# Expert routing on one core: the exponential of the expert weights moved behind the key selections and tied to a gelu

## The chip, the cores and the metric

The kernel runs on one core of a Trainium2 chip. The metric is the device time of one execution in microseconds (us). A core has five engines with a queue each: PE (TensorE: matrix products, weight loads apart as PEld), DVE (VectorE), ACT (ScalarE: activation functions), POOL (GpSimd) and SP (SyncE, which here only issues transfers). Each engine works through its queue strictly in order; semaphores join the queues.

## The reference, cut to what matters

The network has two layers over 256 context and 256 latent tokens of width 1024. Each layer ends in a product-key expert feed-forward block, 16384 experts of which each of 8 heads uses 16 for each token:

```python
s1, i1 = lax.top_k(s[:, :, 0], PEER_TOPK)
s2, i2 = lax.top_k(s[:, :, 1], PEER_TOPK)
cand = (s1[..., :, None] + s2[..., None, :]).reshape(...)
cidx = (i1[..., :, None] * PEER_NKEYS + i2[..., None, :]).reshape(...)
top_s, pos = lax.top_k(cand, PEER_TOPK)
eidx = jnp.take_along_axis(cidx, pos, axis=-1)
g = jax.nn.softmax(top_s, axis=-1)
act = jax.nn.gelu(jnp.einsum('td,thkd->thk', xc, u[eidx]), approximate=False)
coef = g * act
return jnp.einsum('thk,thkd->td', coef, v[eidx])
```

The change concerns the exponential inside `softmax(top_s)`, on 128 tokens x 128 weights at a time.

## The kernel before, in words

The expert block doesn't gather rows of `u`. It multiplies all of them with the tokens, 128 experts in a step, in `u_step`: a step loads one 128x1024 block of `u` (SP, tile `wr`, four buffers), splits it in a high and a low part for exact products (`whi` by ACT, `wlo` by POOL, three buffers each, L364 and L365), runs 24 matmuls of the three partial products into PSUM (`pu`, two buffers in layer 0, three in layer 1), takes the gelu on ACT (`gel`, L538) and stores it in DRAM from the ACT queue. There are 128 steps in a layer (the U stage). In layer 0 they cover 512 tokens, but the first 22 steps only the 256 latent ones, because attention did the context half earlier; in layer 1 they cover 256 tokens.

Beside it `route_tile` works out, for 128 tokens at a time (four tiles in layer 0, two in layer 1), which experts count and with what weight. That is nearly all DVE work: the best 16 of 128 scores for 16 key sets, the sums `cand`, the best 16 of 256 for 8 heads, the subtraction of the maximum (L910, into `e = g[:, 2]`), then for each of the two key indices (x = 0 and 1) three passes over 128x2048 elements (`eq`, L921, L925, L927), then the sum `z`, its reciprocal and the division of `e` (L932 to L934, L941). Three PE transposes (L945, `ptr`) turn the result, DVE casts it (`gT`, L947), and 16 groups of one-hot tiles A and B (L975 to L978) feed matmuls (`pw`) that scatter the weights into a dense matrix, which goes to DRAM by way of ACT (`stg`) and a transfer. The last tile of layer 0 takes a shorter way: `index` turns it into row numbers for gathers in the next stage (the V stage).

The order of PE and of DVE in the U stage is the order in which the program is written out. It is woven by hand: `route_tile` is a generator that yields a planned cost after each piece, and `pace` runs it on at the middle and at the end of each step of U. A tile of dense routing costs 93.5 units by the plan. Layer 0 has 3 x 93.5 + 52 = 332.5 units over 112 steps (its half steps count half), layer 1 has 187 over 120. After the end of each step from step 24 on, layer 0 also writes out one product for the second layer's modulation vectors (`mj`, L166, on DVE), whose operand `wm` comes by an SP transfer.

The order of ACT and of SP isn't written out. A scheduler of the framework orders their instructions by its own model of when operands are ready. `issue_after(ins)` forbids it one thing: an instruction written in that block can't stand ahead of `ins` in their engine's queue. `self.gel` is the latest gelu that `u_step` has written:

```python
self.mm3(p, w, h, t0, t1, range(4))
if mid:
    mid()
self.mm3(p, w, h, t0, t1, range(4, C))
g = self.w.tile([P, T], F32, tag="gel", name="gel", bufs=3)[:, :n]
self.gel = nc.scalar.activation(g, p, AF.Gelu)
nc.scalar.dma_start(self.Gd[l][j][:, t0:t1], g)
```

So a piece of routing that is written in the middle of step j sees the gelu of step j-1, one at the end of step j sees that of step j. ACT holds one set of function tables at a time; exp and gelu are in different sets, so each exponential among the gelus comes with one table load before it and one after it.

Of the kernel before, what the change touches and what calls it, by code (L numbers as in the profile page):

```python
# [14 lines left out]
AF = mybir.ActivationFunctionType  # L15
# [94 lines left out]
class Trunk:  # L110
# [767 lines left out]
    def route_tile(self, l, ps, rp, s, it, Wd):  # L878
        nc = self.nc
# [29 lines left out]
        e = g[:, 2]  # L909
# [9 lines left out]
        for x in range(2):  # L919
            eq = rp.tile([P, HEADS, TOPK, TOPK], F32, tag="cand", name="eq")  # L920
            V.tensor_tensor(eq.rearrange("p h k j -> p (h k) j"),  # L921
                            abf[:, x].rearrange("p h k -> p (h k)")[:, :, None].to_broadcast([P, P, TOPK]),
                            self.iota[:, None, :TOPK].to_broadcast([P, P, TOPK]), op=OP.is_equal)
            yield 2.2
            V.tensor_tensor(eq, eq, sifp[:, :, x, None, :].to_broadcast([P, HEADS, TOPK, TOPK]), op=OP.mult)  # L925
            yield 2.2
            V.tensor_reduce(g[:, x], eq, axis=AX.X, op=OP.add)  # L927
            if x == 0:
                nc.scalar.activation(e, e, AF.Exp)
            yield 2.2  # L930
        z = rp.tile([P, HEADS], F32, tag="z", name="z")
        V.tensor_reduce(z, e, axis=AX.X, op=OP.add)  # L932
        V.reciprocal(z, z)
# [32 lines left out]
        for t0 in range(0, P, TG):  # L966
            stg = rp.tile([P, NK, TG], F32, tag="stg", name="stg", bufs=2)
            for u0 in range(t0, t0 + TG, HB):
# [3 lines left out]
                x = [gT[:, y, u0:u0 + HB, None].to_broadcast(sh) for y in range(4)]  # L972
# [623 lines left out]
```

## Time and profile before

| what | us |
|---|---|
| median of 3 runs | 2804.37 |
| lowest and highest of them | 2802.23, 2816.68 |
| the profiled execution, its own time | 2819.22 |
| its span, first to last instruction | 2817.4 |
| PE busy with matmuls in it | 2644.6 |
| DVE busy | 2080.1 |
| POOL busy | 1300.8 |
| ACT busy | 1176.5 |

All views below are of that one profiled execution, whose own time is 14.85 us above the median of the runs.

### The profile page before, as it was taken

The page shows a single profiled execution, that of the slowest core. Times are in us where ns is not written, and L with a number is a line of the kernel's source. Part 1 is how long each engine was busy: PE and PEld are TensorE (multiplying, and loading weights), DVE is VectorE, ACT ScalarE, POOL GpSimd, SP SyncE. Part 2 cuts the span into 40 slices and gives each one's busy share as a digit, 9 for nine tenths or more (in the row PEclk, how much of TensorE's full clock was granted, in tenths as well). Part 3 has the DMA queues.
Part 4 walks back from the last instruction along what each step waited for, and adds up shares of the span by engine and source line. Part 5 has one row for each costly group of instructions (what it writes and reads, how often), then busy time and mean ns, then how long its engine had stood idle before and what let it go on. Part 6 is the DMA issues. An engine that isn't in the chain of part 4 may idle for free.

```text
span 2817.4 us, 46000 instructions
## 1 busy us (share of the span) xinstructions
PE 2644.6 (94%) x17403; PEld 2407.1 (85%) x17403; DVE 2080.1 (74%) x3689; ACT 1176.5 (42%) x1953; POOL 1300.8 (46%) x730
## 2 busy tenths in 40 slices
PE   8889999999899999999999999987999899999998
PEld 3667898887777777789999999977999799999998
DVE  5898764839958959515988878688939929577776
ACT  3445433434224233333333333464445445444444
POOL 3433440755445445446777763243578688400000
PEclk9989999999999999999999999999999999999999
DMA  7342262557548668558999998314578678888885
GB/s 259 131 133 77 89 215 83 172 191 250 198 165 257 222 228 269 189 185 293 353 358 385 376 346 328 111 47 143 176 214 261 191 221 261 304 284 278 278 278 171
DMA packets 223566, 631.58 MB, mean 224 GB/s; under 512 B 28480, under 2 KB 84464, under 8 KB 218736
## 3 DMA queue, kind: packets, MB, share of 16 engines
q1 hardware_dynamic: 148880, 468.03, 49.0%
q0 software_dynamic: 33888, 109.75, 11.5%
q10 hardware_dynamic: 40576, 50.87, 5.0%
q8 instruction: 136, 2.23, 0.3%
q14 instruction: 86, 0.70, 0.1%
HBM read 535.28 MB, written 93.33 MB: 223 GB/s over the span
## 4 chain that ended last, share of the span: by engine, by line
PE 61%; DVE 25%; DMA 5%; issue 3%; ACT 3%; POOL 3%; SPq 0%; ACTq 0%; DVEq 0%; POOLq 0%
PE y L1169 26%; PE pu L373 7%; PE pu L375 7%; PE pu L374 7%; DVE mj L166 3%; DVE B L977 2%; DVE B L976 2%; DVE A L975 2%; POOL wlo L365 2%; DVE B L978 2%; DMA gr<-Gd 1%; PE pq L373 1%; PE pq L375 1%; PE pq L374 1%; PE pw L958 1%
## 5 line engine op out<-in xcount | busy, mean ns | idle before, releaser
L365 POOL TENSOR_TENSOR wlo<-wr,whi 128x1024 fp32r<-128x1024 f32 x306 | 801.2, 2624 | 697.7 <-ACT whi L364 562.0
L364 ACT ACTIVATE whi<-wr 128x1024 fp32r<-128x1024 f32 x575 | 608.7, 1059 | 905.3 <-PE pu L374 493.9
L1169 PE MATMUL y<-gh,whi 128*128 128x256 f32 (+1 forms) x2072 | 635.3, 309 | 12.8 <-ACT gh L352 11.0
L1169 PE MATMUL y<-gl,whi 128*128 128x256 f32 (+1 forms) x2072 | 639.6, 309 | 4.3 <-DVE gl L353 3.8
L1169 PE MATMUL y<-gh,wlo 128*128 128x256 f32 (+1 forms) x2072 | 638.2, 308 | 0.5 <-DVE wlo L365 0.5
L365 DVE TENSOR_TENSOR wlo<-wr,whi 128x1024 fp32r<-128x1024 f32 x291 | 358.4, 1232 | 294.1 <-ACT whi L364 268.4
L373 PE MATMUL pu<-hh,whi 128*128 128x512 f32 (+1 forms) x1024 | 394.8, 386 | 21.1 <-ACT gel L538 21.1
L1169 PEld LDWEIGHTS y<-gh,whi 128*128 128x128 f32 x2072 | 389.1, 188 | 17.3 <-ACT gh L352 14.8
L1169 PEld LDWEIGHTS y<-gl,whi 128*128 128x128 f32 x2072 | 394.9, 191 | 7.5 <-DVE gl L353 7.3
L1169 PEld LDWEIGHTS y<-gh,wlo 128*128 128x128 f32 x2072 | 390.5, 188 | 0.7 <-DVE wlo L365 0.7
L375 PE MATMUL pu<-hh,wlo 128*128 128x512 f32 (+1 forms) x1024 | 385.7, 377 | 3.7 <-POOL wlo L365 3.7
L374 PE MATMUL pu<-hl,whi 128*128 128x512 f32 (+1 forms) x1024 | 383.5, 375 | 0.0
L373 PE MATMUL pu<-h,whi 128*128 128x256 f32 x1024 | 296.5, 290 | 6.6 <-ACT whi L364 6.6
L375 PE MATMUL pu<-h,wlo 128*128 128x256 f32 x1024 | 290.8, 284 | 7.8 <-POOL wlo L365 7.8
L374 PE MATMUL pu<-h,whi 128*128 128x256 f32 x1024 | 290.0, 283 | 0.0
L373 PEld LDWEIGHTS pu<-hh,whi 128*128 128x128 f32 x1024 | 195.7, 191 | 53.6 <-ACT gel L538 23.0
L375 PEld LDWEIGHTS pu<-hh,wlo 128*128 128x128 f32 x1024 | 195.2, 191 | 41.1 <-POOL wlo L365 4.9
L374 PEld LDWEIGHTS pu<-hl,whi 128*128 128x128 f32 x1024 | 196.1, 192 | 31.6
L166 DVE SCALAR_TENSOR_TENSOR mj<-wm,cb 128x1024 bf16<-128x1024 f32 x128 | 206.1, 1610 | 1.3 <-DMA wm<-in_wmodT 0.9
L375 PEld LDWEIGHTS pu<-h,wlo 128*128 128x128 f32 x1024 | 195.7, 191 | 9.3 <-POOL wlo L365 9.3
L373 PEld LDWEIGHTS pu<-h,whi 128*128 128x128 f32 x1024 | 196.2, 192 | 6.8 <-ACT whi L364 6.8
L352 ACT ACTIVATE gh<-G 128x384 fp32r<-128x384 f32 (+1 forms) x250 | 115.6, 462 | 195.3 <-DVE G L1109 177.7
(378 smaller groups left out, 4907.1 us busy)
## 6 DMA issues: line engine op xcount, KB each, us to landing
wr<-in_uT SPq DMA_DIRECT2D x278, 512.0 KB, 3.9
wr<-in_vT SPq DMA_DIRECT2D x256, 512.0 KB, 5.0
wm<-in_wmodT SPq DMA_DIRECT2D x80, 512.0 KB, 4.0
Wd<-stg POOLq DMA_DIRECT2D x40, 1024.0 KB, 7.7
Gd<-gel ACTq DMA_DIRECT2D x106, 256.0 KB, 2.7
wb<-Wd SPq DMA_DIRECT2D x16, 1536.0 KB, 10.8
gr<-Gd SPq DMA_DIRECT2D x128, 192.0 KB, 6.7
Gd<-gel ACTq DMA_DIRECT2D x172, 128.0 KB, 3.5
```

What stands on the lines that cost most here:

```text
L166: x = nc.vector.scalar_tensor_tensor(j, rs[i], 1.0, self.cb[:, s], op0=OP.mult, op1=OP.mult, accum_out=self.mv[l][n // C][:, n % C, s:s + 1])
L352: self.nc.scalar.activation(hi, x, AF.Copy)
L364: nc.scalar.activation(hi, r, AF.Copy)
L365: (lo_engine or nc.vector).tensor_tensor(lo, r, hi.bitcast(F32), op=OP.subtract)
L373: nc.tensor.matmul(out, whi[:, s], hh[:, c, t0:t1], start=c == 0, stop=False)
L374: nc.tensor.matmul(out, whi[:, s], hl[:, c, t0:t1], start=False, stop=False)
L375: nc.tensor.matmul(out, wlo[:, s], hh[:, c, t0:t1], start=False, stop=c == C - 1)
L975: V.tensor_tensor(Av, io, x[0], op=OP.is_equal)
L976: V.tensor_tensor(Bv[1], io, x[1], op=OP.is_equal)
L977: V.tensor_tensor(Bv[0], Bv[1], x[2], op=OP.mult)
L978: V.tensor_tensor(Bv[1], Bv[1], x[3], op=OP.mult)
L1169: nc.tensor.matmul(y[:, n0:n1], w[:, s], g[:, n0:n1], start=first and x == 0, stop=False, skip_group_check=True)
```

## The change

The exponential leaves the loop over the two key indices and is written once after it, just ahead of the sum that needs it, inside a block that forbids the scheduler to put it ahead of the latest gelu.

```diff
             V.tensor_tensor(eq, eq, sifp[:, :, x, None, :].to_broadcast([P, HEADS, TOPK, TOPK]), op=OP.mult)
             yield 2.2
             V.tensor_reduce(g[:, x], eq, axis=AX.X, op=OP.add)
-            if x == 0:
-                nc.scalar.activation(e, e, AF.Exp)
             yield 2.2
+        with self.tc.issue_after(self.gel.ins):
+            nc.scalar.activation(e, e, AF.Exp)
         z = rp.tile([P, HEADS], F32, tag="z", name="z")
         V.tensor_reduce(z, e, axis=AX.X, op=OP.add)
         V.reciprocal(z, z)
```

## Rows read from the trace of the kernel before

**Rows 1.** The page's first part: busy time of each engine, share, instructions.

```profile
PE 2644.6 (94%) x17403; PEld 2407.1 (85%) x17403; DVE 2080.1 (74%) x3689; ACT 1176.5 (42%) x1953; POOL 1300.8 (46%) x730
```

**Rows 2.** The exponential's line: durations in ns; under it, idle ahead of it.

```profile
L929 ACT ACT_TABLE_LOAD  x6: 1283/1283/1283, 530.7 to 2221.4; - x6
L929 ACT ACTIVATE g<-g x6: 309/310/317, 532.7 to 2231.9; 128x128 f32<-128x128 f32 x6
...
  DVE g L910: 44.7, 6
```

**Rows 3.** Waits: who waited for whom, us in total, times, longest.

```profile
DVE gT L947 <- PE ptr L945: 204.1, 5, 51.9
...
PE pu L373 <- ACT gel L538: 21.1, 4, 8.1
...
PE pu L373 <- ACT whi L364: 6.6, 1, 6.6
```

**Rows 4.** Timeline of ACT, second tile of layer 0: start, duration, idle before.

```profile
731.56 0.58 ACT L538 ACTIVATE gel<-pu 128x512 f32<-128x512 f32 x1
737.00 0.58 ACT L538 ACTIVATE gel<-pu 128x512 f32<-128x512 f32 x1
...
737.97 1.28 ACT L929 ACT_TABLE_LOAD   x1 [0.39 <-ACT gel L538]
752.89 0.31 ACT L929 ACTIVATE g<-g 128x128 f32<-128x128 f32 x1 [13.64 <-DVE g L910]
...
763.81 0.58 ACT L538 ACTIVATE gel<-pu 128x512 f32<-128x512 f32 x1
```

**Rows 5.** Timeline of PE there: the first matmul after its pause.

```profile
755.16 0.79 PE L373 MATMUL pu<-hh,whi 128*128 128x512 f32 x1 [8.11 <-ACT gel L538]
```

**Rows 6.** Stretches there: length, busy us (count) by engine, granted clock, transfers.

```profile
750.00:755.00 5.00, 0.00 (x0) 0.00 (x0) 4.93 (x15) 2.08 (x3) 0.00 (x0) 0.50 0.39 156
755.00:760.00 5.00, 4.84 (x12) 3.83 (x13) 5.00 (x4) 2.49 (x4) 3.87 (x2) 0.53 0.46 141
```

**Rows 7.** Timeline of ACT: gelus around the exponentials of tiles three and four.

```profile
946.29 0.58 ACT L538 ACTIVATE gel<-pu 128x512 f32<-128x512 f32 x1
...
972.01 0.58 ACT L538 ACTIVATE gel<-pu 128x512 f32<-128x512 f32 x1
...
1132.99 0.58 ACT L538 ACTIVATE gel<-pu 128x512 f32<-128x512 f32 x1
...
1155.95 0.58 ACT L538 ACTIVATE gel<-pu 128x512 f32<-128x512 f32 x1
```

**Rows 8.** Timeline of ACT: gelus around the second exponential of layer 1.

```profile
2217.83 0.37 ACT L538 ACTIVATE gel<-pu 128x256 f32<-128x256 f32 x1
...
2220.69 0.36 ACT L538 ACTIVATE gel<-pu 128x256 f32<-128x256 f32 x1
...
2242.79 0.36 ACT L538 ACTIVATE gel<-pu 128x256 f32<-128x256 f32 x1
```

**Rows 9.** Timeline of POOL around the first exponential of each layer.

```profile
530.12 2.40 POOL L365 TENSOR_TENSOR wlo<-wr,whi 128x1024 fp32r<-128x1024 f32 x1 [0.47 <-ACT whi L364]
535.75 29.41 POOL L365 TENSOR_TENSOR wlo<-wr,whi 128x1024 fp32r<-128x1024 f32 x9 [3.23 <-ACT whi L364]
...
2025.90 27.37 POOL L365 TENSOR_TENSOR wlo<-wr,whi 128x1024 fp32r<-128x1024 f32 x9 [3.52 <-ACT whi L364]
```

**Rows 10.** Timeline of ACT: the gelu of step 57 in layer 0.

```profile
807.33 0.58 ACT L538 ACTIVATE gel<-pu 128x512 f32<-128x512 f32 x1
```

**Rows 11.** Timeline of PE: the second tile's transposes.

```profile
811.79 0.49 PE L945 MATMUL ptr<-ident,g 128*128 128x128 f32 x3
```

**Rows 12.** Timeline of DVE: from the second tile's sum to what follows.

```profile
778.16 0.27 DVE L932 TENSOR_REDUCE z<-g 128x8 f32<-128x128 f32 x1
...
779.17 1.22 DVE L166 SCALAR_TENSOR_TENSOR mj<-wm,cb 128x1024 bf16<-128x1024 f32 x1
```

**Rows 13.** Timeline of ACT: the V stage's first gelu, late in layer 0's U stage.

```profile
1173.78 0.42 ACT L1105 ACTIVATE gr<-gr 128x256 f32<-128x256 f32 x1 [6.38 <-DMA gr<-Gd]
```

## The prediction

> **What bounds the kernel now.** I read the page's first part, then the line of the exponential, the waits, the timelines of ACT, PE, DVE and POOL around each of the six exponentials, and stretches of a few us there. PE is busy for 94% of the span [rows 1], so only what makes PE stand still, or run at its lower clock, is worth anything.
>
> In the U stage a step of layer 0 takes 5.44 us from gelu to gelu (737.00 - 731.56 [rows 4]), one of layer 1 2.86 us (2220.69 - 2217.83 [rows 8]). The exponential is cheap: six times a 1.283 us table load and 0.31 us of work. But ACT stood idle 44.7 us in front of the six, waiting for DVE's subtraction L910 [rows 2]. At the second tile ACT loads the tables at 737.97 and can compute only at 752.89 [rows 4]. All that time nothing else on ACT runs, and behind the exponential in its queue stand the gelus, which free PE's accumulators, and the splits `whi`, which feed POOL and PE. PE runs on until both accumulators are full, stands for 8.11 us until the gelu comes [rows 5], and then works at a granted clock of 0.50 to 0.53, the lower of its two levels (1.2 of 2.4 GHz), in a stretch whose predecessor had no matmul [rows 6].
>
> Why is ACT there so early? Gelus counted, the exponential at 752.89 stands behind the gelu of step 46. By the yields it is written at unit 37.0 of a tile (16.8 + 2.2 + 13.6 for the selections and sums, 4.4 for two passes), for the second tile at (93.5 + 37.0)/332.5 x 112 + 11 = step 55.0 (the 11 are the 22 half steps at the start), that is in step 54's last call. The scheduler pulled it eight steps ahead, to where its model holds the subtraction done; the true DVE is later. The other five, counted in the same way, stand behind the gelus of steps 5, 78 and 107, and of 5 and 63 in layer 1: 8 to 20 steps ahead of their place in the text.
>
> Yet DVE isn't the bound. After each of five tiles it waits for PE's transposes, 204.1 us in all [rows 3], because those are held to the text's order. The stall at the exponential is one of order, not of capacity.
>
> **The change part by part.** *The new place.* It is written at unit 45.8 of a tile (8.8 later), for the second tile at 139.3/332.5 x 112 + 11 = 57.9, in step 57's last call, tied to that step's gelu. Worked out likewise, the ties are the gelus of steps 25, 57, 88, 120 in layer 0, and 28, 88 in layer 1. There the operand is long ready: the second tile's subtraction ends when the exponential starts, at 752.9 [rows 4], and gelu 57 runs at 807.33 [rows 10]. So the exponential should stand directly behind its gelu and wait for nothing. The number of table loads stays: one before, one after.
>
> *What goes.* I price each stall by what the gelus around it took beyond the regular step, which holds both PE's pause and its slow clock.
> - Tile 2 of layer 0: 763.81 - 737.00 = 26.81 for three steps, less 16.32: 10.49 us [rows 4].
> - Tile 3: 25.72 - 16.32 = 9.40 us. Tile 4: 22.96 - 16.32 = 6.64 us [rows 7].
> - Second tile of layer 1: 2242.79 - 2220.69 = 22.10 for four steps, less 11.44: 10.66 us [rows 8].
> - First tile of each layer: ACT waited little there, but PE is short of `wlo` and POOL works in one run of nine. POOL's own pause in front of that run is what the exponential costs: 3.23 and 3.52 us where 0.47 is regular [rows 9], so 2.76 + 3.05 = 5.81 us. Bounds: nothing, if DVE's passes slow POOL by as much anyway, and the whole 5.81.
>
> Sum: 10.49 + 9.40 + 6.64 + 10.66 + 5.81 = 43.0 us. The waits bear the kind out: PE lost 21.1 us to late gelus and 6.6 to a late `whi` [rows 3], 27.7 of pure pause, the rest being slow clock and the refilling of `whi` and `wlo`.
>
> *What comes.* ACT spends 2 x 1.28 + 0.31 = 2.9 us at the new places. In layer 0 its idle time in each step covers that: ACT is busy for 42% of the span [rows 1], some 2.3 of 5.44 us. In layer 1's 2.86 us steps `whi` comes up to about 2 us late, and two splits done ahead cover that; without this cover it would cost 2 x 2 = 4 us. Taken: nothing.
>
> DVE now waits for the exponential at the sum L932 instead of at `gT`, a few us sooner in its queue. Behind it stand the four small instructions, one `mj`, and `gT`, which PE's `pw` matmuls wait for. The exponential ends 0.97 + 1.28 + 0.31 = 2.56 us after its gelu starts (load offset from [rows 4]); DVE's four take 1.01 us [rows 12]: the weights are ready 3.6 us after the gelu's start. The second tile's transposes come 811.79 - 807.33 = 4.46 us after it [rows 10, 11], so PE has 0.9 us to spare; tiles 1 and 3 have half a step (2.7 us) more, layer 1's tiles about as little. But the `mj` (1.22 us) that used to run during the wait now lies between; at the second tile it ends at 3.6 + 1.2 = 4.8 us, and `gT` starts up to 1 us later, twice that where POOL slows DVE. I take 1.5 us for this; bounds 0 and 2 us at each of the three tiles that have an `mj`, 6 us.
>
> *What moves later.* The fourth tile's index is ready some 7 us after gelu 120 instead of ahead of it. The first loads of the V stage follow it on SP, and ACT has there one more wait ahead of its time, 6.38 us for `gr` [rows 13]. I expect it to stay in size at a later place. Bounds: 6.4 us won if it vanishes, 6 us lost if it doubles; taken as nothing. Seven steps (38 us) remain to the end of the stage for what the V stage needs.
>
> Sum: 43.0 - 1.5 = 41.5 us off the profiled execution, 2819.2 to 2777.7. That execution lies 14.85 us above the median; stalls aren't likely to be all of that, so I take the same 41.5 off the median: 2804.4 - 41.5 = 2763 us. If all of the 14.85 were stalls, the gain would be 26.7 us, 2778.
>
> **The rivals.**
> - *The transposes wait (part of the gain).* If ACT takes a split between gelu and exponential, or DVE is late, PE stands at the five transposes for up to 2 or 3 us, and its clock may fall. Five times 4 us is 20: a gain of 21, 2783 us. For it: 0.9 us of slack at three of five tiles. Against: `whi` runs ahead of its gelu and not behind it in the regular step. ScalarE: Activation LUTs of the Trainium skill, section "What ACT_TABLE_LOAD costs", adds a drain of 1.38 us to each load of 1.283 us. By that the weights would come about 1.4 us later than by my sum, PE would wait about 0.5 us at three tiles, and the time would be 2765 us.
> - *The load queue stands (slower).* SP works in order. If a `wm` load that waits for the `mj` now behind L932 stands in it ahead of the `u` loads, no `wr` comes while DVE waits. DVE's five waits for `ptr` come to 204.1 us, some 41 each [rows 3], and would lie before the `mj`; four buffers are a cover of 4 x 5.44 = 22 us. Three tiles in layer 0 lose 41 - 22 = 19, plus some 2.4 us of slow clock each (10.49 - 8.11 [rows 4, 5]): 64 us lost, 2763 + 64 = 2827 us. The change turns into a loss where the queue is blocked for over 41.5/3 - 2.4 + 22 = 33 us a tile. Against: in the kernel before, DVE waits as long one `mj` later, and the steps go on regularly (8 from 763.81 to 807.33, 5.44 us each [rows 4, 10]).
> - *No effect to be measured.* If layer 0's V stage starts no sooner than before, because its first loads now follow a later index, layer 0's share goes (10.49 + 9.40 + 6.64 + 2.76 = 29.3 us), and 41.5 - 29.3 = 12.2 us are left: 2792 us. For it: ACT already waits 6.38 us for such a load [rows 13]. Against: 38 us of cover.
>
> **How the numbers follow.** Forecast 2763 us: 0.78, its own range 2750 to 2780 (bounds above: 43.0 + 6.4 = 49 won, and 26.7 less some). Transposes wait, 2783: 0.11. No effect, 2792: 0.07. Load queue, 2827: 0.04. The range 2748 to 2788 leaves the last two cases out, and some of the tails. What a measurement of this kernel can tell from no change is about 0.5%, 14 us. Faster by more takes both first cases and little else: 0.89; within it 0.07; slower 0.04.
>
> **What would show it.** Right: no exponential with more than 1 us of idle ahead on ACT; each directly behind the gelu of steps 25, 57, 88, 120 and 28, 88; the waits of `pu` for `gel` down from 21.1 to a few us; U steps at 5.44 us around steps 46 to 49, 78 to 81 and 107 to 110; still a slow stretch at the first tiles for `wlo`; DVE's long wait at L932, for ACT, no longer at L947. Wrong: waits at L945 for DVE, SP gaps with `wm` at their head, pauses of PE in the same steps for another reason, or a U stage that ends sooner with a V stage that starts no sooner.

## The result, and the profile after

The kernel after takes 2767.15 us (median of 4 runs, 2764.06 to 2778.01), the kernel before 2809.37 us on the same chip (4 runs, 2802.23 to 2816.68: the three that stood ahead of the prediction and a fourth of 2814.37). The ratio is 0.9863, 95% interval 0.9838 to 0.9889: 38.5 us of 2809, between 31 and 46. The medians lie 42.2 us apart because the runs of each kernel fall in two groups some 12 us apart (2802 and 2804, 2814 and 2817 before; 2764 to 2769, and 2778 after), which the two medians mix differently; group by group the kernels differ by 37 us. That is faster by more than the 0.5% that can be told from no change. The forecast was 2763 us, with a range of 2748 to 2788. The profiled execution of after takes 2768.73 us.

The page's first part and its chain of work (shares by engine), to be read against [rows 1]:

```profile
PE 2626.1 (95%) x17403; PEld 2393.4 (86%) x17403; DVE 2081.3 (75%) x3689; ACT 1177.9 (43%) x1953; POOL 1299.3 (47%) x730
...
PE 70%; DVE 18%; DMA 4%; POOL 3%; issue 3%; ACT 3%; ACTq 0%; DVEq 0%; POOLq 0%; SPq 0%
```

No engine has more or fewer instructions. PE is busy for 18.5 us less, 13.0 of it in a stage that the change doesn't touch (below); the chain runs through PE for 70% and through DVE for 18%, in before for 61% and 25%.

The exponential's line in after (durations in ns, then idle ahead of it, then who waited for it: us, times), against [rows 2]:

```profile
L930 ACT ACT_TABLE_LOAD  x6: 1283/1283/1283, 606.2 to 2266.1; - x6
L930 ACT ACTIVATE g<-g x6: 309/310/310, 607.5 to 2267.3; 128x128 f32<-128x128 f32 x6
its engine sat idle before it (us, times) until:
who waited for it (us, times):
  DVE z L932: 210.4, 6
```

The 44.7 us of idle time on ACT are gone: nothing stands under "sat idle". The six exponentials stand behind the gelus of steps 25, 57, 88 and 120 of layer 0 and 28 and 88 of layer 1, as predicted.

The waits of after (us in total, times, longest), against [rows 3]:

```profile
DVE z L932 <- ACT g L930: 210.4, 6, 46.1
...
PE pw L958 <- DVE B L977: 15.4, 8, 3.9
...
DVE gT L947 <- PE ptr L945: 10.9, 5, 3.2
...
PE pu L373 <- ACT gel L538: 1.4, 1, 1.4
```

DVE's long wait has moved from `gT` to the sum and kept its size. PE's wait for late gelus fell from 21.1 us to 1.4. A wait of PE at the transposes (L945) for DVE, which would have been a sign against the prediction, doesn't appear among the waits of after.

Two stretches of after at the place of [rows 6] (length, busy us and count of PE, PEld, DVE, ACT and POOL, granted clock, busy share of the transfer engines, GB/s):

```profile
750.00:755.00 5.00, 5.00 (x24) 4.14 (x23) 5.00 (x21) 1.38 (x3) 2.40 (x1) 1.00 0.75 229
755.00:760.00 5.00, 5.00 (x24) 4.14 (x23) 4.93 (x8) 1.31 (x2) 2.42 (x1) 1.00 0.48 192
```

Where PE stood and then worked at a granted clock of 0.50 to 0.53, it now runs through at 1.00, the upper of its two levels.

**Where the time went.** I counted the gelus in both traces and took the time from one gelu to another, as the prediction did. Positive is time won.

| stretch | before, us | after, us | won | predicted |
| --- | --- | --- | --- | --- |
| layer 0, tile 2, steps 46 to 49 | 26.81 | 16.32 | 10.49 | 10.49 |
| layer 0, tile 3, steps 78 to 88 | 63.80 | 54.54 | 9.26 | 9.40 |
| layer 0, tile 4, steps 107 to 110 | 22.96 | 16.32 | 6.64 | 6.64 |
| layer 1, tile 2, steps 63 to 88 | 83.83 | 74.87 | 8.96 | 10.66 |
| layer 0, first tile, steps 5 to 25 | 73.28 | 73.99 | -0.71 | 2.76 |
| layer 1, first tile, steps 5 to 28 | 70.57 | 69.04 | 1.53 | 3.05 |
| layer 0, new place, steps 57 to 60 | 25.02 | 24.78 | 0.24 | -1.5 |
| layer 1, new places, steps 28 to 33 and 88 to 93 | 42.49 | 44.66 | -2.17 | 0 |
| layer 0, `gr`, steps 112 to 115 | 20.24 | 16.32 | 3.92 | 0 |
| the rest of both U stages | | | -0.26 | 0 |
| sum | | | 37.9 | 41.5 |

The profiled executions differ by 50.5 us, 12.6 more than this sum. 12.8 of that lie in layer 1's V stage, from its U stage's last gelu to the end of the span (376.4 us in before, 363.6 in after). They aren't the change's: the kernel of the first experiment below, with the exponentials at the old places, takes 363.9 us there. The start of the run (-1.7) and the stretch between the two U stages (1.5) make up the other 0.2.

### The profile page after: what moved, and what is told of

Its sections match the earlier page's. It is cut to its first block, busy times and chain, and to the rows that moved or that the text cites. A ratio compares the mean times of both kernels' runs of the same rounds, so it can differ in the third digit from the quotient of the medians.

```text
span 2767.0 us, 46003 instructions
## 1 busy us (share of the span) xinstructions
PE 2626.1 (95%) x17403; PEld 2393.4 (86%) x17403; DVE 2081.3 (75%) x3689; ACT 1177.9 (43%) x1953; POOL 1299.3 (47%) x730
## 4 chain that ended last, share of the span: by engine, by line
PE 70%; DVE 18%; DMA 4%; POOL 3%; issue 3%; ACT 3%; ACTq 0%; DVEq 0%; POOLq 0%; SPq 0%
PE y L1169 25%; PE pu L373 10%; PE pu L375 10%; PE pu L374 10%; DVE B L977 2%; PE pw L958 2%; DVE B L976 2%; DVE A L975 2%; POOL wlo L365 2%; DVE mj L166 2%; DVE B L978 2%; PE pq L373 1%; PE pq L375 1%; PE pq L374 1%; DMA gr<-Gd 1%
```

## The experiments

Each is timed against the kernel before, run beside it. Where a stretch is named, it is from gelu to gelu in that kernel's profile.

**The place alone.** The exponential is written behind both selections, without the tie.

```diff
-            if x == 0:
-                nc.scalar.activation(e, e, AF.Exp)
             yield 2.2
+        nc.scalar.activation(e, e, AF.Exp)
```

> The exponential is written behind the loop, but without the tie to the gelu. Theory (the place in ACT's queue is what counts, and the scheduler puts an instruction where its model holds the operand done): ACT waits for the subtraction as before, about 45 us in front of the six exponentials, and the time is that of the kernel before, within 0.4% (2798 to 2820 us). Rival (the place in the program text does it): the time of the changed kernel, about 2767 us.

Measured: 2804.72 us, ratio 0.9989 (0.9974 to 1.0004). The exponential's line there, durations and the idle time ahead of it:

```profile
L929 ACT ACTIVATE g<-g x6: 309/310/312, 534.5 to 2227.2; 128x128 f32<-128x128 f32 x6
its engine sat idle before it (us, times) until:
  DVE g L910: 44.6, 6
```

The scheduler pulls it back behind the gelus of steps 5, 46, 78, 107 and 5, 63. The place in the text, by itself, does nothing.

**The tie alone.** The exponential stays behind the first selection, tied to the latest gelu.

```diff
             if x == 0:
-                nc.scalar.activation(e, e, AF.Exp)
+                with self.tc.issue_after(self.gel.ins):
+                    nc.scalar.activation(e, e, AF.Exp)
```

> The exponential stays in the loop behind the first key index, and only the tie is added: it stands behind the gelus of steps 22, 54, 85, 117 and 23, 83. Theory: the operand is done there too, so no wait ahead of the exponential, and all of the gain stays, 36 to 42 us; its table loads no longer meet the transposes and the one-hot products of layer 1 (steps 28 to 33, where the changed kernel took 22.8 us and the kernel before 20.8), so it may be up to 3 us faster than the changed kernel. Rival (the late place, just ahead of the sum, is needed): ACT still waits, and half of the gain or more is lost.

Measured: 2761.55 us (2757.72 to 2767.97), ratio 0.983 (0.9804 to 0.9855). It stands behind gelus 22, 54, 85, 117 and 23, 83, and ACT waits ahead of none (nothing stands under "sat idle"):

```profile
L930 ACT ACTIVATE g<-g x6: 310/310/312, 589.5 to 2252.5; 128x128 f32<-128x128 f32 x6
its engine sat idle before it (us, times) until:
who waited for it (us, times):
  DVE z L933: 122.8, 6
```

So the tie carries the whole gain: without it the new place gives nothing, and with it the old place gives all. Its profile loses nothing at layer 1's places of after (28 to 33: 20.72 us for 22.84; 88 to 93: 20.75 for 21.82). The intervals of this kernel and of after overlap.

**One layer alone.** The change for layer 0 only, and for layer 1 only.

```diff
-            if x == 0:
+            if x == 0 and l != 0:
...
+        if l == 0:
+            with self.tc.issue_after(self.gel.ins):
+                nc.scalar.activation(e, e, AF.Exp)
```

> The change in layer 0 alone. Theory: the stalls are separate, so the gains add: the U stage of layer 0 takes 705 us as in the changed kernel (735 before), that of layer 1 435 us as before; about 29 us faster than before. Rival (layer 0's gain is given back, its V stage starting no sooner): less than 10 us faster.

> The change in layer 1 alone. Theory: layer 1's U stage takes 427 us (435 before), layer 0's 735 as before; about 8 us faster than before, 0.3%, not the 13.7 of my sum. Rival (layer 1's share is 13 us or more and was hidden in the profile): 13 to 20 us faster.

Measured: layer 0 alone 2779.87 us, ratio 0.9902 (0.9869 to 0.9935); layer 1 alone 2794.59 us, ratio 0.9961 (0.9939 to 0.9983). The gains, 0.98% and 0.39%, add up to the 1.37% of both. In the stretches, layer 0's U stage takes 704.97 us in the first (704.92 in after) and 732.84 in the second (734.77 in before). Layer 1's takes 425.03 in the second (435.31 in before), but 431.84 in the first, 3.5 less than in before though the change isn't in that layer. So the gains of the layers add up, and a difference of 2 to 4 us between the stages of two single profiles shows nothing by itself.

**No table load, before.** In the kernel before, a copy takes the place of the exponential, which is left out.

```diff
-                nc.scalar.activation(e, e, AF.Exp)
+                nc.scalar.activation(e, e, AF.Copy)
```

> The kernel before with a copy in place of the exponential (the exponential is left out), at the same place in ACT's queue: no table loads, the wait for the subtraction stays. Theory (the wait is the price): the pauses of PE stay at the places of the kernel before; only the load back to gelu (1.28 us, after the wait) leaves the path, so 4 to 10 us faster than before, 2794 to 2800 us. Rival (the switching of tables is the price): 30 us faster or more, near the changed kernel.

Measured: 2813.93 us, ratio 1.0007 (0.9984 to 1.0029): my expected gain of some us didn't come. The copy's line:

```profile
L929 ACT ACTIVATE g<-g x6: 309/309/312, 535.8 to 2231.9; 128x128 f32<-128x128 f32 x6
its engine sat idle before it (us, times) until:
  DVE g L910: 54.4, 6
```

The idle time grew from 44.7 to 54.4 us: the loads ahead of the exponentials had been lying inside the wait for DVE. The loads back to gelu, behind the wait, did cost something: the stalls at steps 46, 78 and 107 of layer 0 came out 3.8 us shorter in all, but steps 5 to 25 and 112 to 115 together 3.3 us longer, so that the U stages take 734.22 and 434.75 us (734.77 and 435.31). On balance, what the exponential costs in the kernel before is the wait and not the tables.

**No table load, after.** The same copy in the kernel after, which leaves the exponential out too.

```diff
         with self.tc.issue_after(self.gel.ins):
-            nc.scalar.activation(e, e, AF.Exp)
+            nc.scalar.activation(e, e, AF.Copy)
```

> The changed kernel with a copy in place of the exponential (left out): what its twelve table loads still cost at the new places. Theory: nothing in layer 0, where ACT has idle time in each step; in layer 1 up to 2 us a tile at steps 28 to 33 and 88 to 93 (22.8 and 21.8 us in the changed kernel, 20.8 before): 0 to 4 us faster than the changed kernel, 2763 to 2768 us. Rival (the loads cost their 15.4 us of ACT wherever they stand): 10 to 15 us faster, 2752 to 2757 us.

Measured: 2768.36 us, ratio 0.985 (0.981 to 0.9891). Layer 0's U stage stays at 704.77 us; layer 1's falls from 427.26 to 423.44, with 2.08 us of it at steps 28 to 33 and 1.11 at 88 to 93. What two table loads cost at a place without a wait is seen only where steps are 2.86 us long, and not everywhere there: in the kernel with the tie alone they stand behind gelus 23 and 83, and steps 23 to 28 and 83 to 88 take 14.08 us each, as short as without loads (14.24 and 14.08 here).

**The exponential later still.** One work unit later (2.0 in the order's measure), and the transposes right behind the weights.

```diff
+        if not (l == 0 and it == 3):
+            yield 2.0
         with self.tc.issue_after(self.gel.ins):
             nc.scalar.activation(e, e, AF.Exp)
...
         V.tensor_scalar(e, e, WSC, None, op0=OP.mult)
-        yield 2.0
```

> The changed kernel with the exponential, the sum and the division written directly ahead of the transposes, so that nothing lies between. This doubles the disputed wait. Theory (the weights are ready 3.6 us after the gelu's start, that is some 4.5 us after the end of PE's step): PE waits for DVE at the five transposes, about 4.5 us where they come at the end of a step (tile 2, both of layer 1) and 1.9 us in the middle (tiles 1 and 3), 17 us in all, and some slow clock behind the long ones: 15 to 25 us slower than the changed kernel, 2782 to 2792 us. Rival (PE finds other work, or the transposes have slack): within 5 us of the changed kernel.

Measured: 2791.05 us, ratio 0.9919 (0.9889 to 0.9948), 16 us above after by the ratios. Its waits of PE:

```profile
PE ptr L946 <- DVE g L943: 14.4, 5, 4.0
...
PE pw L959 <- DVE B L979: 6.9, 9, 2.7
```

The rival that the prediction priced at 4 us a tile is real if one asks for it: five transposes wait 14.4 us, and the U stages take 10.4 us more than in after (9.12 and 1.30). The other 6 us of the ratio don't lie in the U stages; the profiled execution has layer 1's V stage at the slower of two rates (376 us, told of at the end), which is 12 us longer than in after and would cover them, but it is one execution.

**Short passes in the first tile.** The index selections of tile 0 cover one head of eight; this kernel leaves out seven eighths of that tile's selection.

```diff
+            H = 1 if it == 0 else HEADS
...
+            if it == 0:
+                V.memset(g[:, x], 0.0)
...
-            V.tensor_tensor(eq, eq, sifp[:, :, x, None, :].to_broadcast([P, HEADS, TOPK, TOPK]), op=OP.mult)
+            V.tensor_tensor(eq[:, :H], eq[:, :H], sifp[:, :H, x, None, :].to_broadcast([P, H, TOPK, TOPK]), op=OP.mult)
...
-            V.tensor_reduce(g[:, x], eq, axis=AX.X, op=OP.add)
+            V.tensor_reduce(g[:, x, :H], eq[:, :H], axis=AX.X, op=OP.add)
```

> The changed kernel, where the first tile of each layer makes its three passes for each key index over one head of eight (the indices of the other seven are set to zero, so seven eighths of that selection are left out). Theory (at the first tiles DVE's passes slow POOL's splits, and that is the whole excess there): steps 5 to 25 of layer 0 take 68 us (74.0 in the changed kernel), steps 5 to 28 of layer 1 take 65 us (69.0). Rival (the excess is of another kind, as transfers): 72 to 74 and 68 to 69 us.

Measured: 2767.01 us in one run. In layer 1 the first tile came out as expected (65.5 us for steps 5 to 28), in layer 0 not: steps 5 to 25 took 75.24 us for the 68 expected, with one stall of 10.29 us at step 11. ACT's timeline there (start, duration, idle before it):

```profile
554.97 1.06 ACT L364 ACTIVATE whi<-wr 128x1024 fp32r<-128x1024 f32 x1 [8.97 <-DMA wr<-in_uT]
```

and SP's queue in the same stretch, 520 to 620 us:

```profile
SPq L163 <- DVE mj L166: 12.8, 1, 12.8
```

A `wm` load waits for a buffer that DVE frees with an `mj`, and the `wr` loads of the unit steps stand behind it. That is the prediction's rival of the load queue, once. The same stretch of SP's queue has it, shorter, in after (first line) and, shorter still, in before (second line; the profile puts that wait down to the sum `z`, which starts as the `mj` ends):

```profile
SPq L163 <- DVE mj L166: 8.4, 1, 8.4
```

```profile
SPq L163 <- DVE z L932: 4.2, 1, 4.2
```

So the stand of the queue isn't new in after; it has doubled. In before one `whi` of ACT waits 2.95 us for its `wr` there:

```profile
564.25 1.06 ACT L364 ACTIVATE whi<-wr 128x1024 fp32r<-128x1024 f32 x1 [2.95 <-DMA wr<-in_uT]
```

**The side work later.** Two kernels in which the modulation products begin at step 28 instead of 24: the tie alone, and the short passes.

```diff
-M0 = 24
+M0 = 28
```

> The exponential tied to the latest gelu at its old place (behind the first of the two selections), and the side work of layer 0 (the modulation products mj with their loads wm) starts at unit step 28 instead of 24, so that SP's queue has no wm load behind a product that VectorE has not reached while tile 0's selection passes run. Theory 'SP's queue stands once in layer 0's first tile': the stall of about 6 to 7 us that steps 5 to 25 hold in the kernel after goes, that stretch falls from 74 to 68 to 71 us, and the run ends 2 to 4 us below the kernel with the tie alone (2757 to 2760 by its median of 2761.6). Rival 'VectorE's passes slow GpSimd's splits there and nothing else does': the stretch stays at 73 to 75 us and the time at 2760 to 2764. Third way: the four modulation steps displaced to the end of the stage push V's start of layer 0 back, and the time rises by 3 to 8 us.

> The kernel after with tile 0's index selections cut to one head of eight (the other heads' indices are zero, so this kernel leaves out seven eighths of that tile's selection) and the side work of layer 0 starting at step 28 instead of 24. With the passes short, GpSimd has no VectorE work beside it; with the later side work SP's queue has no wm load that waits. Theory 'both the passes and the queue hold the first tile': steps 5 to 25 of layer 0 take 67 to 69 us, 5 to 7 below the kernel after and the kernel with the short passes alone (74.0 and 75.2). Rival 'the queue alone': the same figure as the kernel with the late side work and full passes, within 1 us. Rival 'neither': 73 us or more.

Measured: with full passes 2762.1 us (2754.28 to 2774.57), ratio 0.9834 (0.9808 to 0.9861); with short ones 2756.95 us in one run. In neither does `wm` wait for `mj` in that stretch. Steps 5 to 25 of layer 0 take 71.47 and 67.76 us. POOL's timeline in the first of them, and then in the second (run of splits, idle before it):

```profile
537.06 29.26 POOL L365 TENSOR_TENSOR wlo<-wr,whi 128x1024 fp32r<-128x1024 f32 x9 [0.47 <-ACT whi L364]
566.70 2.41 POOL L365 TENSOR_TENSOR wlo<-wr,whi 128x1024 fp32r<-128x1024 f32 x1 [0.37 <-ACT whi L364]
```

```profile
536.38 2.40 POOL L365 TENSOR_TENSOR wlo<-wr,whi 128x1024 fp32r<-128x1024 f32 x1 [0.47 <-ACT whi L364]
539.26 2.41 POOL L365 TENSOR_TENSOR wlo<-wr,whi 128x1024 fp32r<-128x1024 f32 x1 [0.48 <-ACT whi L364]
```

With full passes nine splits take 29.26 us, though each found its operands ready; with short ones 2.40 each, in a rhythm of 2.88. The nine aren't evenly slow: four take 4.3 to 4.5 us and five 2.4. Part of DVE's timeline in the kernel with full passes, and POOL's beside it:

```profile
545.84 4.39 DVE L921 TENSOR_TENSOR eq<-abf,iota 128x2048 f32<-128x2048 f32 x1
550.27 4.37 DVE L925 TENSOR_TENSOR eq<-eq,sif 128x2048 f32<-128x2048 f32 x1
554.67 2.29 DVE L927 TENSOR_REDUCE g<-eq 128x128 f32<-128x2048 f32 x1
```

```profile
548.05 4.44 POOL L365 TENSOR_TENSOR wlo<-wr,whi 128x1024 fp32r<-128x1024 f32 x1
552.44 4.43 POOL L365 TENSOR_TENSOR wlo<-wr,whi 128x1024 fp32r<-128x1024 f32 x1
```

The ends alternate: the split before these at 548.09, the pass L921 at 550.23, a split at 552.49, the pass L925 at 554.64, a split at 556.87, each some 2.2 us behind the last, about what either takes by itself (2.40 for a split; 2.29 for L921 in the kernel before at 1153.58, with no split beside it). It looks as if the passes over two tensors and the splits took turns, while the sum over one tensor (L927) takes 2.29 us beside a split too.

So the first tile of layer 0 splits up: 67.76 us with neither, 3.71 more for DVE's full passes, and 2.62 more with the side work at its old place (74.09 in the kernel with the tie alone). How the 2.62 divide isn't shown: SP's queue stands there, but the later start also moves the products themselves, and in after two of them (`mj` at 555.05, 3.39 us, and at 560.57, 1.22 us) run beside splits that take 3.38 us each. Nor do the parts simply add: with short passes and the side work at its old place it was 75.24 us.

The expected time of the kernel with later side work was missed: the 3.7 us won in its U stages against the tie alone (1125.77 for 1129.46) don't show in its median. Neither it nor the tie alone is told from after by the times alone.

## Why the prediction was right, and which terms were off

**Right in its mechanism.** The cost was ACT's wait ahead of its time, not the exponential and not its tables: the wait kept, the loads taken away, gives 1.0007; the wait taken away, the loads kept, gives 0.983. Both sides of the rival "no effect" fell: layer 0's share alone is worth 0.98%, and the V stage of layer 0 starts with the end of the U stage, as before (752.7 us from its last gelu to layer 1's first, 754.2 before).

**The four big stalls** were sized by the regular step: 37.19 us predicted, 35.35 measured. The one that is off, 10.66 to 8.96 in layer 1, was taken from four steps. Over those four 10.71 us were won, but the 21 steps behind them took 1.75 us longer than in before, so part of that stall had been made up again there.

**The first tiles** are the term that failed: 5.81 predicted, 0.82 measured. The prediction named the bound "nothing, if DVE's passes slow POOL by as much anyway", and took the other end. POOL's pause did go in after, but the run behind it got slower:

```profile
537.57 28.82 POOL L365 TENSOR_TENSOR wlo<-wr,whi 128x1024 fp32r<-128x1024 f32 x8 [0.47 <-ACT whi L364]
568.12 7.13 POOL L365 TENSOR_TENSOR wlo<-wr,whi 128x1024 fp32r<-128x1024 f32 x3 [1.73 <-ACT whi L364]
```

Eight splits in 28.82 us, where [rows 9] has nine in 29.41. The experiments give two causes, 3.71 us for DVE's passes and 2.62 for the side work at its old place. The kernel with the tie and later side work, which has the passes alone, takes 71.47 us in steps 5 to 25, the kernel before 73.28: at most these 1.81 us were to be won of the 2.76, and they aren't all the exponential's, since SP's queue stands in before too. In after the queue stands twice as long, and nothing is won. In layer 1 1.53 us of 3.05 were won; short passes there make steps 5 to 28 another 3.54 us shorter (65.50 for 69.04), so DVE's passes hold that tile too.

**ACT at the new places.** In layer 0 the step covers the loads, as predicted. ACT's timeline of after at the second tile (start, duration):

```profile
799.25 0.58 ACT L538 ACTIVATE gel<-pu 128x512 f32<-128x512 f32 x1
799.85 1.28 ACT L930 ACT_TABLE_LOAD   x1
...
801.14 0.31 ACT L930 ACTIVATE g<-g 128x128 f32<-128x128 f32 x1
...
804.80 1.28 ACT L538 ACT_TABLE_LOAD   x1
806.09 0.60 ACT L538 ACTIVATE gel<-pu 128x512 f32<-128x512 f32 x1
```

In layer 1 the term "taken: nothing" was 2.17, of a bound of 4. Single profiles scatter here: with the loads at these steps five kernels take 43.0 to 44.7 us, without them seven take 40.0 to 43.5 (on average 44.1 and 41.7). ACT and then POOL of after there:

```profile
2059.22 0.36 ACT L538 ACTIVATE gel<-pu 128x256 f32<-128x256 f32 x1
2059.60 1.28 ACT L930 ACT_TABLE_LOAD   x1
...
2060.90 0.31 ACT L930 ACTIVATE g<-g 128x128 f32<-128x128 f32 x1
2061.22 1.28 ACT L538 ACT_TABLE_LOAD   x1
2062.52 0.38 ACT L538 ACTIVATE gel<-pu 128x256 f32<-128x256 f32 x1
```

```profile
2063.93 7.94 POOL L365 TENSOR_TENSOR wlo<-wr,whi 128x1024 fp32r<-128x1024 f32 x3 [2.14 <-ACT whi L364]
```

POOL stands 2.14 us for a late `whi` where 0.45 is regular: the two splits done ahead didn't cover it. With the table loads taken out, the loss goes (41.47 us).

**The transposes.** DVE's chain in after at the second tile (start, duration, idle before it), and PE's transposes:

```profile
801.48 0.28 DVE L932 TENSOR_REDUCE z<-g 128x8 f32<-128x128 f32 x1 [17.93 <-ACT g L930]
...
802.51 1.22 DVE L166 SCALAR_TENSOR_TENSOR mj<-wm,cb 128x1024 bf16<-128x1024 f32 x1
...
804.23 0.96 DVE L947 CAST gT<-ptr 128x768 f16<-128x768 f32 x1 [0.49 <-PE ptr L945]
```

```profile
803.70 0.49 PE L945 MATMUL ptr<-ident,g 128*128 128x128 f32 x3
```

The weights are ready at 802.60, 3.35 us after the gelu's start (predicted 3.6), and the transposes come at 4.45 (predicted 4.46). The `mj` ends at 803.73, before the transposes end, and `gT` still waits 0.49 us for PE: the 1.5 us for the `mj` ahead of it weren't paid, and the stretch came out 0.24 us shorter. The rule of the Trainium skill that was weighed, ScalarE: Activation LUTs, section "What ACT_TABLE_LOAD costs", with a drain of 1.38 us on each load, isn't borne out: the exponential starts 0.01 us after its load's 1.28 us, at 801.14, and the gelu at 806.09 likewise; ahead of the first load, too, the gelu ends at 799.83 and the load starts at 799.85.

**The load of `gr`.** I expected the wait "to stay in size at a later place". It shrank:

```profile
1199.33 0.42 ACT L1105 ACTIVATE gr<-gr 128x256 f32<-128x256 f32 x1 [1.74 <-DMA gr<-Gd]
```

1.74 us for the 6.38 of [rows 13], and steps 112 to 115 won 3.92 us, inside the named bound of 6.4. I didn't test why it shrank; that its loads are issued some 25 us later, behind a later index, is what the trace shows. The wait isn't the whole of the stretch either: in before the two table loads of another exponential (at 1175.43 and 1176.95) follow `gr` between the same two gelus; in after `gr` comes behind gelu 122 and they behind gelu 123 (at 1205.18 and 1208.01), and steps 120 to 127 take as long as before (37.3 us).

**The median.** "Stalls aren't likely to be all of that" fits the traces: the V stage of layer 1, which the change doesn't touch, took some 12.8 us longer in that profiled execution than in after, close to the 14.85 us between it and the median. Which part of the 14.85 lies there isn't shown, as the runs of the median have no profile.

**Luck in the sum.** The U stages won 37.9 us for the 41.5 forecast, but the terms were further off than that. The first tiles fell short by 4.99 us, the stalls by 1.84 and the new places in layer 1 by 2.17, and the 3.92 at `gr`, taken as nothing, and 1.74 at the transposes happened to make up most of it.

## What to carry to other kernels

When an engine waits long for an operand, count where the text put the waiting instruction: if it stands many steps ahead of that, the scheduler's model was wrong about the operand's engine, and a tie to the latest instruction of the main loop can be worth more than moving lines (here 0.983 against 0.9989). Price the stall by the regular step around it, over enough steps to see what is made up again. Where another engine was slow beside the stall, ask first whether it would be slow without it.

## What the runs showed of the hardware that wasn't expected

**The V stage has two rates at one granted clock.** A stretch of 50 us of layer 1's V stage in the kernel before, and then in after (length, busy us and count by engine, granted clock, busy share of the transfer engines, GB/s):

```profile
2500.00:2550.00 50.00, 50.00 (x427) 50.00 (x426) 35.63 (x54) 23.73 (x37) 0.00 (x0) 1.00 0.81 283
```

```profile
2500.00:2550.00 50.00, 50.00 (x444) 50.00 (x443) 36.52 (x56) 25.27 (x37) 0.00 (x0) 1.00 0.85 285
```

PE is busy throughout at a granted clock of 1.00 in both, and does 427 matmuls in one and 444 in the other, 117.1 and 112.6 ns each. Of the twelve profiles of this case, nine show 443 or 444 and three 427 (before, the late exponential, and the tie with later side work); their stage takes about 376 us from the U stage's last gelu to the end, the others' 363. Since before and the first experiment fall on different sides, it isn't the place of the exponential. The two groups in the times of one kernel, some 12 us apart, would fit a rate that changes from execution to execution, but only the profiled executions show the stage itself. What decides is open.

**DVE's passes and POOL's splits hold each other up.** A split took 2.40 us alone and 4.3 to 4.5 beside a pass over two tensors, and that pass took 4.4 us where it takes 2.29 alone. A product `mj`, 1.22 us elsewhere, took 3.39 in after while POOL was in a split, and the split that began during it took 3.38. The sum over one tensor took its 2.29 us beside a split as well. Why isn't shown; the alternating ends above are what the trace has.
